# A hybrid decoder layer in fp32: the second feed-forward product done as seven block products instead of eight

## The chip, the core and the metric

One core of a Trainium2 chip runs the whole layer in one launch. TensorE multiplies 128 x 128 weight tiles with up to 512 columns into PSUM; VectorE (DVE), ScalarE (ACT) and GpSimd (POOL) do the element work between SBUF tiles of 128 partitions, and SyncE (SP) issues the transfers between HBM and SBUF. GpSimd does not touch PSUM in this kernel. The metric is device time of one launch in microseconds, the median of several runs; lower is better.

## What is computed

One decoder layer for a prompt of 2048 tokens and 8 sample tokens, model width 1024, feed-forward width 2816. Cut to what matters here:

```python
x = x + rmsnorm(merged @ p['w_out'], p['g_mix_post'])
hf = rmsnorm(x, p['g_ffn_pre']) @ p['w_ffn_in']                     # 1024 -> 2 * 2816
f = (jax.nn.silu(hf[..., :D_FF]) * hf[..., D_FF:]) @ p['w_ffn_out']  # 2816 -> 1024
x = x + rmsnorm(f, p['g_ffn_post'])
```

Everything ahead of this (state space branch, pooling branch, attention to memory, gates) stays as it is.

## The kernel before

Activations lie transposed: channels on partitions, tokens along the columns. The 2048 tokens are four quarters q of 512 columns. The 8 sample tokens ride along with quarters 0 and 1, four each, so that these are 516 columns wide (`fwidth`, L1261) and are worked in two blocks of 258; quarters 2 and 3 are 512 wide. `SB` pairs the quarters: superblock 0 is quarters 0 and 1, superblock 1 is quarters 2 and 3.

Each fp32 product is made of three TensorE passes over fp32r operands: `split` (L170) makes a rounded part on ACT and the rest on DVE (or on POOL), and the passes are high by high, high by low and low by high. So every loaded operand tile costs one ACT and one DVE instruction before TensorE can use it.

The last 1435 us are three stretches.

**First product, superblock 0 and then 1** (`ffn_in`, L1309, pool "half"). Both quarters of a superblock are multiplied together by a scheme of seven block products (Winograd's form of Strassen): `sums` (L1270) makes seven combinations of the normalized input and stores them to `d_S`, `left` (L1297) loads and splits them into 56 `S` tiles, and for each of the 22 tiles f_ of the feed-forward width `w_pair` (L261) combines the weights on DVE. Superblock 0 uses 22 x 7 x 4 x 3 x 2 = 3696 matmuls of 258 columns, superblock 1 1848 of 512. At the end of each f_, ACT takes the sigmoid, POOL multiplies f0 by it (L1386), DVE multiplies by the other half (L1388), and the two tiles go out to `d_f` (L1389). `take` and `plus` (L1340, L1343) move results out of PSUM between the block products.

**Second product** (`ffn_out`, L1402, pool "down"), the plain way: for each quarter, `load_f` (L1392) brings 22 tiles of f through four `xr` buffers and splits them into `f` tiles; then for each of 8 output tiles m, 22 x 3 matmuls for each of two blocks of columns. The blocks are 258 wide in quarters 0 and 1 and 256 wide in 2 and 3; quarter 3 is done in two halves one after the other, with the weights loaded twice. In all 4 x 8 x 22 x 3 x 2 = 4224 matmuls. Weights `fo` come in chunks of 8, 8 and 6 blocks of 128 x 128 from `in_w_all`, three chunks ahead (`prefetch`, L297, `AHEAD`), through four `wr`, `wh` and `wl` buffers (L281 to L294). The last 8 chunks are split on POOL.

**Finish** of a quarter (`finish`, L1428): the sum of squares gives the norm's scale (`rsqrt_rows`, `spread`), then for 8 tiles DVE multiplies (L1442), POOL or DVE adds the residual loaded from `d_x2` (L1443), and the tile is stored (L1444). It runs in the background of the next quarter: `step` (L221) takes one piece of it, `flush` all that is left.

The order of instructions on each engine is fixed when the kernel is built: a scheduler walks a simulated timeline and takes what is ready, by priority, which is the order of the program unless `tc.high_priority(offset=...)` pulls a part ahead (`URGENT` 300, `LEAD` 700). On the chip each engine works its list strictly in that order. SP issues all transfers in order too, and a transfer whose buffer is not free holds those behind it. A pool that is opened after another has been closed takes the same SBUF: the "down" tiles lie where the "half" tiles were, and each waits for the tiles that it overlaps. `xr`, `tmp`, `wr`, `wh`, `wl` and `rb` are outside of these pools.

## Time and profile before

| | us |
|---|---|
| median of 3 runs | 3132.57 (3129.24 to 3135.39) |
| the profiled execution | 3137.2 |
| its span, first to last instruction | 3135.4 |
| first product, superblock 0, first matmul | 1693.8 |
| last matmul of the first product | 2588.4 |
| last matmul of the second product | 3117.3 |

The mean granted TensorE clock is 0.976 of full speed. The profile counts times from the start of the span. In a row of a timeline the columns are start, duration, engine, line and operation, output and input tiles, shape and count; the bracket is the time that the engine stood idle before it and what ended that. Engines: PE is the matmuls, PEld the weight loads beside them, SPq the issue of transfers. Matmuls are pipelined: their own durations (0.28 us at 258 columns) overlap, so the pace is read from start to start, or from a stretch of the chain and the number of matmuls in it.

### The profile page before, as it was taken

Reading aid. Unit: us, or ns where it says so; the run is one execution under the profiler, and the core shown is the slowest. Engines: PE = TensorE matmul, PEld = TensorE weight load, DVE = VectorE, ACT = ScalarE, POOL = GpSimd, SP = SyncE. Lnnn points to the kernel's source line nnn. Section 1 sums busy time; section 2 is a strip of 40 time slices with the busy share of each in tenths; the row PEclk is TensorE's granted clock in tenths of the full one; section 3 lists DMA queues with packets and bytes.
Section 4 is the critical chain, followed back from the end, with each engine's and each line's share of the span. In section 5 each row is a group of like instructions: output and inputs, shape, how many; then the busy total and the mean of one; then the engine's idle time right before and its main releaser. Section 6 shows DMA issues by size and latency. Waiting matters only on the chain. (4 is left out here: it accounts for less than half of the span.)

```text
span 3135.4 us, 47779 instructions
## 1 busy us (share of the span) xinstructions
PE 2984.2 (95%) x18631; PEld 2671.6 (85%) x18631; DVE 1886.8 (60%) x3121; ACT 1197.7 (38%) x2017; POOL 739.2 (24%) x630
## 2 busy tenths in 40 slices
PE   7989998799999999989996999999999999999997
PEld 6778877689997888878885999998888878999997
DVE  8776756664538645485566855557666654345364
ACT  4532434322445333452333433335333334324343
POOL 2564245532245122450222000000000000011012
PEclk9989999899999999999997999999999999999999
DMA  6344333663434433354374732225222225445575
GB/s 213 110 160 140 121 122 115 165 212 98 126 118 155 129 107 124 122 170 144 101 222 138 230 116 80 82 82 172 85 81 81 81 91 169 154 154 176 156 251 172
DMA packets 205715, 432.78 MB, mean 138 GB/s; under 512 B 47472, under 2 KB 55216, under 8 KB 205488
## 3 DMA queue, kind: packets, MB, share of 16 engines
q1 hardware_dynamic: 205488, 429.72, 44.1%
q8 instruction: 146, 2.39, 0.3%
q14 instruction: 81, 0.66, 0.1%
HBM read 362.82 MB, written 66.49 MB: 137 GB/s over the span
## 5 line engine op out<-in xcount | busy, mean ns | idle before, releaser
L171 ACT ACTIVATE wh<-wr 128x1024 fp32r<-128x1024 f32 (+1 forms) x460 | 458.5, 997 | 1058.0 <-PE pa L117 816.8
L117 PE MATMUL pa<-S,wh 128*128 128x258 f32 (+1 forms) x3696 | 831.2, 321 | 29.2 <-ACT S L171 20.5
L172 DVE TENSOR_TENSOR wl<-wr,wh 128x1024 fp32r<-128x1024 f32 x372 | 432.2, 1163 | 516.8 <-ACT wh L171 503.0
L117 PEld LDWEIGHTS pa<-S,wh 128*128 128x128 f32 x3696 | 615.4, 190 | 87.5 <-ACT S L171 22.0
L117 PE MATMUL pa<-h,wh 128*128 128x512 f32 (+2 forms) x2560 | 664.6, 355 | 18.7 <-ACT tmp L1037 7.4
L117 PE MATMUL pa<-S,wl 128*128 128x258 f32 (+1 forms) x1848 | 586.7, 320 | 0.3 <-DVE wl L172 0.3
L117 PEld LDWEIGHTS pa<-h,wh 128*128 128x128 f32 x2560 | 436.4, 191 | 85.4 <-ACT tmp L1037 7.6
L117 PE MATMUL pa<-br,wh 128*128 128x512 f32 (+2 forms) x1848 | 472.8, 352 | 15.4 <-ACT wh L171 8.6
L117 PE MATMUL pa<-f,wh 128*128 128x258 f32 (+1 forms) x2816 | 470.0, 284 | 5.5 <-ACT f L171 3.2
L117 PE MATMUL pa<-h,wl 128*128 128x512 f32 (+2 forms) x1280 | 419.5, 354 | 0.0
L117 PEld LDWEIGHTS pa<-f,wh 128*128 128x128 f32 x2816 | 401.6, 191 | 7.6 <-ACT f L171 4.3
L117 PEld LDWEIGHTS pa<-S,wl 128*128 128x128 f32 x1848 | 349.7, 189 | 27.4 <-DVE wl L172 0.5
L117 PEld LDWEIGHTS pa<-br,wh 128*128 128x128 f32 x1848 | 312.5, 191 | 63.6 <-ACT wh L171 8.6
L172 POOL TENSOR_TENSOR wl<-wr,wh 128x1024 fp32r<-128x1024 f32 (+1 forms) x88 | 214.3, 2438 | 442.0 <-ACT wh L171 331.2
L117 PE MATMUL pa<-f,wl 128*128 128x258 f32 (+1 forms) x1408 | 313.0, 283 | 4.5 <-DVE wl L172 4.5
L117 PE MATMUL pa<-br,wl 128*128 128x512 f32 (+2 forms) x924 | 296.0, 351 | 0.5 <-DVE wl L172 0.5
L117 PEld LDWEIGHTS pa<-h,wl 128*128 128x128 f32 x1280 | 230.1, 191 | 33.4
L1386 POOL TENSOR_TENSOR tmp<-tmp,ev 128x516 f32<-128x516 f32 (+1 forms) x44 | 59.2, 1345 | 840.1 <-ACT tmp L1385 840.1
L117 PEld LDWEIGHTS pa<-f,wl 128*128 128x128 f32 x1408 | 230.7, 190 | 4.8 <-DVE wl L172 4.8
L117 PEld LDWEIGHTS pa<-br,wl 128*128 128x128 f32 x924 | 164.7, 191 | 23.7 <-DVE wl L172 0.8
L172 DVE TENSOR_TENSOR wl<-wt,wh 128x1024 fp32r<-128x1024 f32 x88 | 107.6, 1223 | 108.3 <-ACT wh L171 108.1
L1341 ACT ACTIVATE ev<-pa 128x258 f32<-128x258 f32 (+1 forms) x198 | 89.3, 454 | 180.0 <-PE pa L117 160.2
(329 smaller groups left out, 3494.1 us busy)
## 6 DMA issues: line engine op xcount, KB each, us to landing
wr<-in_w_all SPq DMA_DIRECT2D x408, 512.0 KB, 3.6
ops<-d_ops SPq DMA_DIRECT2D x112, 256.0 KB, 3.8
xr<-in_x_t SPq DMA_DIRECT2D x80, 256.0 KB, 3.7
xr<-d_x SPq DMA_DIRECT2D x72, 256.0 KB, 4.0
wr<-in_w_all SPq DMA_DIRECT2D x40, 384.0 KB, 3.3
d_f<-tmp SPq DMA_DIRECT2D x44, 258.0 KB, 4.4
xr<-d_f SPq DMA_DIRECT2D x44, 258.0 KB, 3.8
d_f<-tmp SPq DMA_DIRECT2D x44, 256.0 KB, 2.9
```

Source lines behind the costliest of these rows:

```text
L117: self._done(self.nc.tensor.matmul(*a, **k))
L171: S.activation(dst_hi, src, AF.Copy)
L172: (eng or V).tensor_tensor(dst_lo, src, f(dst_hi), SUB)
L1341: both(lambda u, s: S.activation(dst[:, s], X[u][:, :w], AF.Copy))
L1386: G.tensor_tensor(f0[:, :n], f0[:, :n], p1[:, :n], MUL)
```

## The change

The second product of a superblock is done as a two-by-two block product in seven products instead of eight: the rows of blocks are the two quarters, the inner blocks the two halves of the feed-forward width (11 tiles each), the columns of blocks the two halves of the model width (4 tiles each).

- **The products** (`ffn_out`): for each superblock, seven products in the order 0, 1, 5, 4, 6, 2, 3, each of 4 output tiles by 11 inner tiles by 3 passes. In superblock 0 each is two matmuls of 258 columns, in superblock 1 one of 512; only the last product of superblock 1 is done in two halves of 256, with its weights loaded twice. Partial results stay in 16 `z` tiles: product 0 is copied out by ACT, the others are added on DVE (`plus`); the squares for the norm are taken by ACT from SBUF and added on POOL, in the last product on DVE.
- **Sums of f** (end of `ffn_in`): the first product now walks f_ as j, j + 11, and after every pair POOL makes four combinations from the tiles at hand (one after the even tile, three after the odd one), 2 a tile on average, 88 in all. They are stored to `d_fs`, late: after the first block product of the next f_ (`put_sums`).
- **Sums of the weights** (`out_weights`): in the background of superblock 1's first product, 11 pieces of 512 columns; each loads four blocks through the four `xr` buffers, makes four combinations on POOL (44 in all) and stores four to `d_T`.
- **Loading** (`load_f`): 11 tiles for each product instead of 22 for each quarter; the loads of the next product are woven in, three after each output tile. The first product's loads are pulled ahead by `LEAD`.
- **Weights**: key `w2`, in chunks of 8 blocks (the last of 4), 6 a product, from `in_w_all` for products 0 to 2 and from `d_T` for the others. The last 6 chunks are split on POOL.
- **Finish**: quarter 0 (or 2) is finished after product 2, beside product 3; quarter 1 beside the next superblock; quarter 3 by halves. Its gain now comes in the multiply (one `scalar_tensor_tensor` on DVE). The residual of quarter 3 is loaded once for both halves into `z` tiles.
- `sums` uses one `tmp` tile less.

```diff
-FCH = (8, 8, 6)
-FOFF = (0, 8, 16)
+KF = NF // 2
+NPC = 4 * KF
+FPC = tuple(min(8, NPC - c) for c in range(0, NPC, 8))
+FORD = tuple(x for j in range(KF) for x in (j, j + KF))
+OUT_ORDER = (0, 1, 5, 4, 6, 2, 3)
+OUT_BLOCK = {0: (0, 0), 1: (1, 0), 2: (1, 1)}
+OUT_SUM = {4: 0, 5: 1, 6: 2, 2: 3}
 SB = ((0, 1), (2, 3))
 KH = KD // 2
...
     wo = [("wo", m) for m in range(KD)]
-    fo = [("fo", c, m) for m in range(KD) for c in range(len(FCH))]
...
     for sb in range(len(SB)):
-        seq += [("f1", f) for f in range(NF)]
-    for q in range(NQ):
-        seq += fo
-    seq += fo
+        seq += [("f1", f) for f in FORD]
+    for sb in range(len(SB)):
+        for i in OUT_ORDER:
+            seq += [("w2", i, c) for c in range(len(FPC))] * len(out_halves(sb, i))
     return seq
 
 
+def out_halves(sb, i):
+    if sb == 0:
+        return [[(0, HW_ // 2), (HW_ // 2, HW_ // 2)]]
+    return [[(0, TQ // 2)], [(TQ // 2, TQ // 2)]] if i == OUT_ORDER[-1] else [[(0, TQ)]]
...
-            "ev": 4, "S": 56, "f": 52, "z": 8}
+            "ev": 4, "S": 56, "f": 44, "z": 16, "st": 3}
...
+    d_fs = dram([len(SB), 4, KF, P, HW_], "d_fs")
+    d_T = dram([4, len(FPC), P, KD * P], "d_T")
...
+        elif key[0] == "w2":
+            src = d_T[key[1] - 3, key[2]] if key[1] > 2 else I["w_all"][_WIDX[("fo",) + OUT_BLOCK[key[1]] + key[2:]]]
...
-        split(hi[:, :n], lo[:, :n], raw[:, :n], G if key[0] in ON_POOL or i >= len(seq) - KD else V)
+        split(hi[:, :n], lo[:, :n], raw[:, :n], G if key[0] in ON_POOL or i >= len(seq) - len(FPC) else V)
...
-            s1, s2, s3, s4 = (slot("tmp")[:, :n] for _ in range(4))
+            s1, s2, s4 = (slot("tmp")[:, :n] for _ in range(3))
+            s3 = A[1, 0]
...
-        for f_ in range(NF):
+        late = []
+
+        def put_sums():
+            for i, j, t in late:
+                nc.sync.dma_start(d_fs[sb, i, j, :, :n], t[:, :n])
+            late.clear()
+
+        for at, f_ in enumerate(FORD):
...
             if nb == 2:
                 product(X, 0, B11, True)
                 take(p1)
+                put_sums()
                 product(Z, 1, B21, True)
...
+            j = at // 2
+            if at % 2 == 0:
+                a21, s3 = f1, slot("tmp")
+                G.tensor_tensor(s3[:, :n], f0[:, :n], f1[:, :n], SUB)
+                late.append((2, j, s3))
+            else:
+                G.tensor_tensor(a21[:, :n], a21[:, :n], f1[:, :n], ADD)
+                G.tensor_tensor(s3[:, :n], f1[:, :n], s3[:, :n], SUB)
+                G.tensor_tensor(f0[:, :n], f0[:, :n], s3[:, :n], SUB)
+                late += [(0, j, a21), (1, j, s3), (3, j, f0)]
             step()
-
-    def load_f(q, n):
-        ft = []
-        for f_ in range(NF):
+        put_sums()
+
+    def out_weights():
+        for c in range(len(FPC)):
+            for o in range(0, FPC[c] * P, 512):
+                W = []
+                for r in range(2):
+                    for m in range(2):
+                        t = slot("xr")
+                        nc.sync.dma_start(t[:, :512], I["w_all"][_WIDX[("fo", r, m, c)]][:, o:o + 512])
+                        W.append(t[:, :512])
+                b11, b12, b21, b22 = W
+                G.tensor_tensor(b22, b22, b12, SUB)
+                G.tensor_tensor(b12, b12, b11, SUB)
+                G.tensor_tensor(b11, b11, b22, ADD)
+                G.tensor_tensor(b21, b21, b11, SUB)
+                yield
+                yield
+                for i, t in enumerate((b21, b12, b11, b22)):
+                    nc.sync.dma_start(d_T[i, c, :, o:o + 512], t)
+                for _ in range(3):
+                    yield
+
+    def load_f(sb, i, out):
+        n = fwidth(SB[sb][0])
+        for k in range(KF):
+            if i in OUT_SUM:
+                src = d_fs[sb, OUT_SUM[i], k]
+            else:
+                src = d_f[SB[sb][i // 2], k + KF * (i > 0)]
             raw = slot("xr")
-            nc.sync.dma_start(raw[:, :n], d_f[q, f_, :, :n])
+            nc.sync.dma_start(raw[:, :n], src[:, :n])
             hi, lo = slot("f", F32R), slot("f", F32R)
             split(hi[:, :n], lo[:, :n], raw[:, :n])
-            ft.append((hi, lo))
-        return ft
-
-    def ffn_out(ft, bl, z, st):
+            out.append((hi, lo))
+            yield
+
+    def ffn_out(sb, i, ft, bl, C, st, loader):
+        u, c11, c12, c22 = C
         sl = slice(bl[0][0], bl[-1][0] + bl[-1][1])
-        for m in range(KD):
+
+        def plus(dst, src, ps):
+            for p_, (o, nn) in zip(ps, bl):
+                V.tensor_tensor(dst[:, o:o + nn], src[:, o:o + nn], p_[:, :nn], ADD)
+
+        def squares(row, t):
+            if st[row] is None:
+                st[row] = slot("st")
+                S.activation(st[row][:, :fwidth(SB[sb][0])], t[:, :fwidth(SB[sb][0])], AF.Square)
+                return
+            sq = slot("tmp")
+            S.activation(sq[:, sl], t[:, sl], AF.Square)
+            (G if sb == 0 or i != 3 else V).tensor_tensor(st[row][:, sl], st[row][:, sl], sq[:, sl], ADD)
+
+        for m in range(KH):
             ps = [psum() for _ in bl]
-            for c in range(len(FCH)):
-                hi, lo = wget("fo", c, m)
-                for j in range(FCH[c]):
-                    i = FOFF[c] + j
-                    ws = slice(j * P, (j + 1) * P)
-                    ah, al = ft[i]
-                    for p_, (o, nn) in zip(ps, bl):
-                        T.matmul(p_[:, :nn], lhsT=hi[:, ws], rhs=ah[:, o:o + nn], start=i == 0, stop=False)
-                        T.matmul(p_[:, :nn], lhsT=hi[:, ws], rhs=al[:, o:o + nn], start=False, stop=False)
-                    for p_, (o, nn) in zip(ps, bl):
-                        T.matmul(p_[:, :nn], lhsT=lo[:, ws], rhs=ah[:, o:o + nn], start=False, stop=i == NF - 1)
-            if len(z) <= m:
-                z.append(slot("z"))
-            sq = st if m == 0 else slot("tmp")
-            for p_, (o, nn) in zip(ps, bl):
-                zs = slice(o, o + nn)
-                S.activation(sq[:, zs], p_[:, :nn], AF.Square)
-                S.activation(z[m][:, zs], p_[:, :nn], AF.Copy, scale=g_fpost[:, m:m + 1])
-            if m > 0:
-                V.tensor_tensor(st[:, sl], st[:, sl], sq[:, sl], ADD)
+            for k in range(KF):
+                c, j = divmod(m * KF + k, 8)
+                if j == 0:
+                    wpiece[0] = wget("w2", i, c)
+                hi, lo = wpiece[0]
+                ws = slice(j * P, (j + 1) * P)
+                ah, al = ft[k]
+                for p_, (o, nn) in zip(ps, bl):
+                    T.matmul(p_[:, :nn], lhsT=hi[:, ws], rhs=ah[:, o:o + nn], start=k == 0, stop=False)
+                    T.matmul(p_[:, :nn], lhsT=hi[:, ws], rhs=al[:, o:o + nn], start=False, stop=False)
+                for p_, (o, nn) in zip(ps, bl):
+                    T.matmul(p_[:, :nn], lhsT=lo[:, ws], rhs=ah[:, o:o + nn], start=False, stop=k == KF - 1)
+            fast.append(tc.high_priority(offset=URGENT if sb and i == 3 else 0))
+            fast[-1].__enter__()
+            if i == 0:
+                u.append(slot("z"))
+                for p_, (o, nn) in zip(ps, bl):
+                    S.activation(u[m][:, o:o + nn], p_[:, :nn], AF.Copy)
+            elif i == 1:
+                c11.append(slot("z"))
+                plus(c11[m], u[m], ps)
+                squares(0, c11[m])
+            elif i == 5:
+                plus(u[m], u[m], ps)
+            elif i == 4:
+                c12.append(slot("z"))
+                plus(c12[m], u[m], ps)
+            elif i == 6:
+                c22.append(slot("z"))
+                plus(c22[m], c12[m], ps)
+                plus(u[m], u[m], ps)
+                squares(1, c22[m])
+            elif i == 2:
+                plus(c12[m], c12[m], ps)
+                squares(0, c12[m])
+            else:
+                plus(u[m], u[m], ps)
+                squares(1, u[m])
+            fast.pop().__exit__(None, None, None)
+            for _ in range(3):
+                next(loader, None)
             step()
+
+    wpiece = [None]
+    fast = []
+    last_x = []
...
-            xt = slot("xr")
-            load_half(xt, d_x2[:, k], q)
+            if q + 1 < NQ:
+                xt = slot("xr")
+                load_half(xt, d_x2[:, k], q)
+            elif len(last_x) > k:
+                xt = last_x[k]
+            else:
+                xt = slot("z")
+                last_x.append(xt)
+                load_half(xt, d_x2[:, k], q)
             zk = z[k][:, sl]
-            V.tensor_tensor(zk, zk, rb, MUL)
+            V.scalar_tensor_tensor(zk, zk, g_fpost[:, k:k + 1], rb, MUL, MUL)
             (V if q + 1 == NQ and k % 2 else G).tensor_tensor(zk, zk, xt[:, sl], ADD)
             nc.sync.dma_start(O["y_t"][q, :, k, sl.start:e], z[k][:, sl.start:e])
             if own(q):
...
         if sb + 1 < len(SB):
             background.append(second_scale(NQ - 1))
             background.append(sums(sb + 1))
+        else:
+            background.append(out_weights())
         ffn_in(sb, got)
         flush()
     second.__exit__(None, None, None)
 
     down = tc.tile_pool(name="down", bufs=1, reuse_waits="tile")
     stage[0] = down.__enter__()
-    slot("z")
-    for q in range(NQ):
-        n = fwidth(q)
-        ft = load_f(q, n)
-        z = []
-        st = slot("tmp")
-        for bl in ([[(0, n // 2), (n // 2, n // 2)]] if q + 1 < NQ else [[x] for x in HALVES]):
-            ffn_out(ft, bl, z, st)
-            flush()
-            background.append(finish(q, z, st, bl))
+    for tag in ("f", "z", "st"):
+        slot(tag)
+    plan = [(sb, i) for sb in range(len(SB)) for i in OUT_ORDER]
+    ft = []
+    with tc.high_priority(offset=LEAD):
+        run(load_f(*plan[0], ft))
+    for at, (sb, i) in enumerate(plan):
+        if i == OUT_ORDER[0]:
+            C, st = ([], [], [], []), [None, None]
+        nxt = []
+        loader = load_f(*plan[at + 1], nxt) if at + 1 < len(plan) else iter(())
+        for bl in out_halves(sb, i):
+            ffn_out(sb, i, ft, bl, C, st, loader)
+            if i == 2:
+                background.append(finish(SB[sb][0], C[1] + C[2], st[0], bl))
+            elif i == 3:
+                flush()
+                background.append(finish(SB[sb][1], C[0] + C[3], st[1], bl))
+        run(loader)
+        ft = nxt
     flush()
     down.__exit__(None, None, None)
 
```

## Rows read from the trace of the kernel before

**Rows 1.** The page, part 1: busy time, share of the span, instructions.
```profile
PE 2984.2 (95%) x18631; PEld 2671.6 (85%) x18631; DVE 1886.8 (60%) x3121; ACT 1197.7 (38%) x2017; POOL 739.2 (24%) x630
```

**Rows 2.** The chain that ended last, in time: start us, us, what.
```profile
2173.09 411.75 PE pa L117 x1776
...
2585.58 2.83 PE pa L117 x11
...
2617.19 124.55 PE pa L117 x1036
2741.75 0.85 PE pb L117 x12
...
2749.31 1.30 PE pb L117 x12
2750.61 120.30 PE pa L117 x1001
...
2879.79 115.54 PE pa L117 x975
```

**Rows 3.** Busy time by stretch: from:to, its length, busy us (instructions), clock, DMA.
```profile
core 0: us, PE busy (x) PEld busy (x) DVE busy (x) ACT busy (x) POOL busy (x), PEclk, DMA share, GB/s
1800.00:2100.00 300.00, 300.00 (x2510) 300.00 (x2510) 166.61 (x278) 109.46 (x194) 19.89 (x15) 1.00 0.32 91
2250.00:2550.00 300.00, 300.00 (x1297) 243.13 (x1296) 186.85 (x233) 99.85 (x138) 19.39 (x15) 1.00 0.25 81
2590.00:2617.00 27.00, 23.03 (x152) 21.38 (x152) 16.54 (x24) 13.31 (x22) 1.32 (x1) 0.87 0.76 223
2592.00:2596.00 4.00, 2.30 (x10) 2.31 (x11) 3.46 (x6) 0.58 (x2) 0.00 (x0) 0.56 0.87 285
2996.00:3061.00 65.00, 60.45 (x491) 60.25 (x491) 42.39 (x54) 27.84 (x40) 13.13 (x8) 0.95 0.71 233
3061.00:3117.00 56.00, 56.00 (x477) 56.00 (x476) 24.70 (x43) 22.38 (x32) 20.35 (x12) 1.00 0.58 191
```

**Rows 4.** Timeline of POOL and of DVE in the first product, superblock 1.
```profile
2224.95 1.29 POOL L1386 TENSOR_TENSOR tmp<-tmp,ev 128x512 f32<-128x512 f32 x1 [18.17 <-ACT tmp L1385]
2244.41 1.30 POOL L1386 TENSOR_TENSOR tmp<-tmp,ev 128x512 f32<-128x512 f32 x1 [18.17 <-ACT tmp L1385]
...
2243.36 0.69 DVE L172 TENSOR_TENSOR wl<-wr,wh 128x512 fp32r<-128x512 f32 x1 [6.93 <-ACT wh L171]
2243.97 0.68 DVE L1380 TENSOR_TENSOR tmp<-tmp,pa 128x512 f32<-128x512 f32 x1
2244.69 1.57 DVE L1388 TENSOR_TENSOR tmp<-tmp,ev 128x512 f32<-128x512 f32 x1
```

**Rows 5.** Instructions by line and shape from 1700 on: count, busy, mean ns, idle before.
```profile
L172 DVE TENSOR_TENSOR wl<-wr,wh 128x1024 fp32r<-128x1024 f32 x118 | 145.3, 1231 | 135.9 <-ACT wh L171 135.8
...
L172 DVE TENSOR_TENSOR f<-xr,f 128x516 fp32r<-128x516 f32 x44 | 29.4, 694 | 16.2 <-ACT f L171 16.0
...
L1442 DVE TENSOR_TENSOR z<-z,rb 128x516 f32<-128x516 f32 x16 | 20.9, 1378 | 1.2 <-ACT rb L372 1.2
```

**Rows 6.** Timeline of DVE where the first product ends.
```profile
2591.38 1.66 DVE L1388 TENSOR_TENSOR tmp<-tmp,ev 128x512 f32<-128x512 f32 x2
```

**Rows 7.** Timeline of DVE beside quarter 3's first half: quarter 2 is finished.
```profile
3006.73 11.48 DVE L1442 TENSOR_TENSOR z<-z,rb 128x512 f32<-128x512 f32 x8
3018.14 2.28 DVE L172 TENSOR_TENSOR wl<-wr,wh 128x1024 fp32r<-128x1024 f32 x1
```

**Rows 8.** Timeline of the tail, after the last matmul of the second product.
```profile
3117.33 0.38 ACT L1422 ACTIVATE tmp<-pa 128x256 f32<-128x256 f32 x1 [7.04 <-PE pa L117]
...
3122.83 2.74 DVE L1442 TENSOR_TENSOR z<-z,pb 128x256 f32<-128x256 f32 x8 [1.18 <-PE pb L117]
...
3132.38 0.42 DVE L1443 TENSOR_TENSOR z<-z,xr 128x256 f32<-128x256 f32 x1 [2.41 <-DMA xr<-d_x]
```

**Rows 9.** Transfers between 2996 and 3061.
```profile
DMA packets 5587, 15.12 MB, mean 233 GB/s; under 512 B 625, under 2 KB 625, under 8 KB 5582
```

More of the change, by code (lines that the diff above doesn't have):

```diff
@@ L81, in _weight_plan @@
     for sb in range(len(SB)):
-        seq += [("f1", f) for f in range(NF)]
-    for q in range(NQ):
-        seq += fo
-    seq += fo
-    return seq
+        seq += [("f1", f) for f in FORD]
+    for sb in range(len(SB)):
+        for i in OUT_ORDER:
+            seq += [("w2", i, c) for c in range(len(FPC))] * len(out_halves(sb, i))
+    return seq
+def out_halves(sb, i):
+    if sb == 0:
+        return [[(0, HW_ // 2), (HW_ // 2, HW_ // 2)]]
+    return [[(0, TQ // 2)], [(TQ // 2, TQ // 2)]] if i == OUT_ORDER[-1] else [[(0, TQ)]]
 _SEQ = _weight_plan()
-_STORED = [k for k in dict.fromkeys(_SEQ) if k[0] not in ("KT", "V", "f1")]
+_STORED = [k for k in dict.fromkeys(_SEQ) if k[0] not in ("KT", "V", "f1", "w2")]
 _STORED += [(k, f) for f in range(NF) for k in ("fa", "fb")]
+_STORED += [("fo", r, n, c) for c in range(len(FPC)) for r in range(2) for n in range(2)]
 _WIDX = {k: i for i, k in enumerate(_STORED)}
@@ L97, in _ncols @@
         return NB * P
-    if key[0] == "fo":
-        return FCH[key[1]] * P
+    if key[0] == "w2":
+        return FPC[key[2]] * P
     return KD * P
@@ L1601, in _pack @@
         else:
-            o = FOFF[key[1]] * P
-            v = kt(a["w_ffn_out"][0][o:o + FCH[key[1]] * P, key[2] * P:(key[2] + 1) * P])
+            _, r, n, c0 = key
+            v = []
+            for t in range(8 * c0, 8 * c0 + FPC[c0]):
+                m, k = n * KH + t // KF, r * KF + t % KF
+                v.append(a["w_ffn_out"][0][k * P:(k + 1) * P, m * P:(m + 1) * P])
+            v = np.concatenate(v, axis=1)
         w_all[i, :, :v.shape[1]] = v
```

3 lines of the change are left out of this document (2 added, 1 removed).

## Prediction

> **What bounds the kernel now.** I read the page first: matmuls fill 95% of the span, DVE 60%, POOL 24% [rows 1]. Then the chain of waits: over the last third it is matmul after matmul, broken only at seams [rows 2]. So TensorE's stream sets the time, and what counts is the number of matmuls, their pace and the holes. The chain gives the pace: 124.55 / 1036 = 0.1202 us a matmul of 258 columns, 115.54 / 975 = 0.1185 at 256, 411.75 / 1776 = 0.2318 at 512 [rows 2]; 512 columns in one matmul are 2% cheaper than in two. Busy time by stretch shows that inside the stages TensorE never stops while DVE is at 56% (superblock 0) and 62% (superblock 1) and POOL at 6 to 7% [rows 3].
>
> The holes of the second product come from the same views. The last matmul of the first product ends at 2588.4, the tail begins at 3117.3 [rows 2, 8]: 528.9 us. Its 4224 matmuls at the two paces are 2112 x 0.1202 + 2112 x 0.1185 = 504.1, and the small matmuls of the finishes 2.15 for a quarter, 7 for all with the shorter later ones [rows 2]. That leaves 17.8 us of holes. At the start, 2588.4 to 2617.2, 152 matmuls ran [rows 3], worth 18.3 of 28.8: 10.5 lost, partly to a halved clock (granted 0.56 from 2592 to 2596, the low level being 1.2 GHz) after TensorE had stood. The rest, some 7, is mostly one seam at 2996 to 3061: 4.5 us idle and a clock of 0.95 [rows 3]. There DVE does quarter 2's eight multiplies in one burst of 11.5 us, the weight split behind it is done only at 3020.4, itself stretched to 2.28 us from 1.23 [rows 5, 7], and in halves a chunk of weights lasts only 8 x 3 x 0.1185 = 2.8 us, three chunks 8.5: less than the burst.
>
> **What is removed.** After the change superblock 0 takes 7 x 4 x 11 x 3 x 2 = 1848 matmuls of 258: 222.1 us. Superblock 1 takes 792 of 512, 183.6, and 264 of 256, 31.3. With the same 7 us for the finishes: 444.0 against 511.1. So **67.1 us** leave the bounding engine, of which 63 are the eighth product. I take the paces as they are: the first product already uses both forms with as many weight loads.
>
> **Start of the second product.** 11 tiles of f instead of 22, pulled ahead. But the "down" tiles lie on the "half" tiles, and `f` now comes first, over `wt` and `ev` (sizes from the code): tiles k = 2 and 3 cover the `ev` buffers, which the last multiplies of the first product read until 2593.0 [rows 6]. So TensorE can run k = 0 and 1, then waits from about 2590 for a split of some 1.4 us (ACT, then DVE 0.69 [rows 5]) behind 2593.0: 4 us, and after standing the clock may fall as it did. Bounds 4 to 11; I take **7**, 3.5 less than now.
>
> **Added to the first product, on POOL.** 88 sums of f and 44 of weights; a POOL operation of this size takes 1.30 us [rows 4]. In superblock 1 that is 4 a tile f_ beside the one there: 6.5 us of a period of 2244.41 - 2224.95 = 19.5 [rows 4]. POOL holds that. What it does to DVE is the point: while POOL ran from 2244.41 to 2245.71, a DVE multiply of two SBUF tiles took 1.57 instead of 0.69, an operation that reads PSUM kept its 0.68 [rows 4, 5]. So an added POOL operation costs DVE up to 0.88 us if it meets such work: 4 x 0.88 = 3.5 on 0.62 x 19.5 = 12.1, or 15.6 of 19.5. DVE stays below TensorE and has stretches of 6.9 us of waiting in each period [rows 4], but a PSUM tile may be cleared late now and then. Queued behind: DVE's f0 multiply waits for POOL's product, which can stand behind a piece of `out_weights` (four sums, 5.2 us, which wait for their loads); behind that multiply stand weight splits and `plus`. Not less than nothing, at most about 20 us (0.5 us for each of 44 tiles); I take **4**, as the f1 weights are split a whole tile ahead. The sums are needed only in the next stage, and their stores go out one block product later, so SP's queue does not wait on POOL; the loads and stores for the weights use `xr`, idle there, with transfers at 0.25 of the engines' time [rows 3].
>
> The Trainium skill, "GPSIMD Engine Reference", 1. Specifications, says that GpSimd shares its SBUF interfaces with VectorE and contends with DVE instructions of two SBUF inputs; the 1.57 us agrees. Taken to its end (all of 132 x 1.3 = 172 us taken from DVE, an estimate by that page) DVE would stand at 89% in superblock 1, which changes no term but is what the last rival prices.
>
> **Inside the second product.** Splits of f rise from 88 to 154 (ACT and DVE, 0.69 each on DVE [rows 5]), weight columns fall from 112,640 to 84,480 (1.23 per 1024), adds out of PSUM are new (56, about 0.8 each). A product lasts 31 us; DVE does 11 x 0.69 + 5.5 x 1.23 + 4 x 0.8 = 18 of it. A finish adds 11 us of multiplies (1.38 each beside POOL [rows 5]) and 3 of norm: 32, about the product's length. Such finishes fall beside product 3 of superblock 0, product 0 of superblock 1, and product 3 of superblock 1. In the first two a chunk lasts 5.6 to 5.8 us, so three ahead cover the burst: 2 us each at most. The last one runs in halves as now, with three chunks for 8.5 us again and POOL's splits among POOL's adds. I take the 7 that the kernel loses today, 3 for the two seams, and 4 for loads that come closer together: **14**, bounds 4 and 30.
>
> **Tail.** Now 18.1 us from the last matmul to the end of the span, and its last add waits for a transfer of the residual [rows 8]. After: 5.5 to the first multiply as now, plus 0.4 as the add and the square now follow each other; twelve DVE operations of 0.34 to 0.42, some 4.5; 2.6 from the last add's end to the end. 13.0; I take **13.5**, bounds 13 and 18.1 (residual not landed).
>
> **Sum**, against the profiled execution's span of 3135.4: 2588.4 + 4 + 7 + 444.0 + 14 + 13.5 = 3070.9, that is 64.5 less. The profiled execution stands 4.6 above the median of the runs (3137.2 to 3132.57) and 1.8 of it lies outside the span, which the change leaves; the gain goes off the median: 3132.57 - 64.5 = **3068**. All low bounds: 2588.4 + 0 + 4 + 444 + 4 + 13 = 3053.4, so 3050.6 us. All high: 2588.4 + 20 + 11 + 444 + 30 + 18.1 = 3111.5, so 3108.7.
>
> **Rivals.**
> - *The second product starves.* The same bytes and more DVE work go into 85% of the time. In the last product of superblock 1 about 11.6 MB must move (weights twice 2.9 less what was fetched ahead, quarter 2's residual and result, quarter 3's residual, half its result) in 31.3 us of matmuls, 370 GB/s, where the busiest long stretch moved 233 [rows 9]. At 233 this is 50 us instead of 31.3 + 13.5: 5 late, and as much at each of the two other finishes, with the clock falling at each (3 us as at 2996 [rows 3]): 20 to 45 us given back, 3088 to 3113. For it: the stall of [rows 7] exists already. Against it: stretches in between have DVE at 58%, so the spill is absorbed.
> - *Nothing waits.* Seams covered, first product untouched: 3042 to 3050.
> - *The gain does not come* (the product is not shorter, because the paces rise as the number falls): to give 67.1 us back, 2904 matmuls would have to be 23 ns slower each; the first product's pace speaks against it. 3125 to 3140.
> - *Slower: POOL stops the first product.* If every added POOL operation's 0.88 us lands on TensorE, not on DVE's idle time, 132 x 0.88 = 116 us are lost: 3068 - 4 + 116 = 3180. It decides from 0.52 us an operation on (68.5 / 132). It needs DVE without slack; the 6.9 us of waiting in each period [rows 4] speak against it.
>
> The Trainium skill, "HBM Reference", Specifications (TRN2), gives about 425 GB/s to a core that streams alone. By it the 370 GB/s of the first rival would fit and its transfer part be nothing; no stretch of this length in the trace comes near, so I keep the rival.
>
> **How the numbers follow.** Forecast (3050 to 3088) 0.68; starving (3088 to 3113) 0.20; nothing waits 0.06; gain does not come 0.02; slower 0.04. The range takes in the forecast, and the starving case up to 3100, which leaves out some 0.18: 3049 to 3100. 0.2%, or 6 us, is about what a measurement tells from no change. Faster 0.94, same 0.02, slower 0.04.
>
> **What would show it.** Matmuls on the tile `f`: 1848 of 258, 792 of 512, 264 of 256, at the same paces. The last matmul on `S` at most 10 us later than 2588.4. DVE multiplies of L1388's kind longer than 0.69 in more places, POOL near 33% in superblock 1. The first `f` product idle near 4 us. The stall in the last product as now. Tail 13 to 14 us without a wait for the residual. Wrong if TensorE shows idle time inside the first product, or several us at each product of the second.

## The result

The changed kernel takes 3098.35 us (median of 4 runs, 3095.52 to 3101.12) against 3131.81 for the kernel before on the same chip (3129.24 to 3135.39): a ratio of 0.9892 (95% interval 0.9875 to 0.9909). It is faster, as the interval lies below 1, and inside the stated range, but the gain is 33.5 us where 64.5 were forecast. The profiled execution has a span of 3093.7.

The table splits each profiled execution at four events read from the timeline of TensorE: the first matmul on a tile `S`, the first one of 512 columns on `S` (superblock 1 begins), the start of the last one on `S`, and the start of the last matmul on `f`. "Second" is from the last `S` to the last `f`, the tail from there to the end. The start of the first product itself lies between 1686 and 1701 in these executions, though next to nothing ahead of it was changed; so spans differ by that, and the columns are compared, not the spans. A column is one execution each: where kernels share an edit, theirs differ by up to 2.4 us. The medians of e1 to e10 were taken beside runs of the kernel before with medians of 3135.05 to 3136.09.

| kernel | start | superblock 0 | superblock 1 | second | tail | span | median of its runs |
|---|---|---|---|---|---|---|---|
| before | 1693.8 | 458.3 | 436.1 | 528.8 | 18.4 | 3135.4 | 3131.81 |
| after | 1686.1 | 463.4 | 461.2 | 466.6 | 16.4 | 3093.7 | 3098.35 |
| e1_no_wsum | 1693.5 | 464.6 | 441.6 | 467.9 | 16.4 | 3084.0 | 3084.35 |
| e2_no_fsum | 1692.2 | 459.5 | 452.0 | 467.8 | 16.6 | 3088.1 | 3087.48 |
| e3_neither | 1700.6 | 457.7 | 437.9 | 468.4 | 16.5 | 3081.1 | 3076.46 |
| e4_wtraffic | 1692.6 | 464.5 | 443.4 | 466.5 | 16.8 | 3083.8 | 3086.40 |
| e5_pool_only | 1689.0 | 463.1 | 453.5 | 467.3 | 16.6 | 3089.5 | 3096.74 |
| e6_pinned | 1691.5 | 462.2 | 440.4 | 467.9 | 16.6 | 3078.6 | 3083.18 |
| e7_finish_behind | 1695.4 | 462.7 | 441.2 | 467.8 | 15.3 | 3082.4 | 3083.70 |
| e8_late_stores | 1698.6 | 460.4 | 436.6 | 468.2 | 16.8 | 3080.6 | 3082.20 |
| e9_all | 1696.9 | 462.7 | 437.0 | 466.6 | 16.0 | 3079.2 | 3077.78 |
| e10_later | 1692.5 | 461.6 | 437.4 | 458.3 | 22.1 | 3071.9 | 3079.42 |

From before to after: second product -62.2, tail -2.0, superblock 0 +5.1, superblock 1 +25.1. That is -34.0 without the accident of the start, and the medians say -33.5. The second product gave what was forecast; the first product took half of it back.

The page of the changed kernel, part 1, to be read against [rows 1]: TensorE works 61 us less, POOL 254 more.

```profile
PE 2922.8 (94%) x17311; PEld 2570.1 (83%) x17311; DVE 1999.4 (65%) x3220; ACT 1186.1 (38%) x1973; POOL 993.1 (32%) x784
```

Busy time by stretch, columns as in [rows 3]: superblock 0, the seam between the superblocks, superblock 1, the start of the second product, two stretches inside it, and its end.

```profile
1800.00:2100.00 300.00, 299.86 (x2507) 299.66 (x2506) 190.55 (x283) 108.94 (x195) 69.33 (x46) 1.00 0.40 121
2150.00:2180.00 30.00, 25.00 (x122) 20.43 (x121) 23.89 (x37) 14.80 (x25) 10.67 (x4) 0.94 0.71 207
2250.00:2550.00 300.00, 287.55 (x1214) 230.31 (x1214) 197.68 (x223) 93.28 (x131) 115.60 (x74) 0.98 0.45 155
2612.00:2632.00 20.00, 15.53 (x100) 14.73 (x101) 13.65 (x17) 9.18 (x16) 5.88 (x4) 0.83 0.74 228
2632.00:2818.00 186.00, 186.00 (x1551) 186.00 (x1549) 110.85 (x159) 87.37 (x130) 15.60 (x10) 1.00 0.62 199
2864.00:3037.00 173.00, 172.77 (x773) 141.28 (x774) 105.79 (x132) 77.67 (x111) 27.12 (x18) 1.00 0.67 213
3037.00:3062.00 25.00, 18.64 (x159) 18.43 (x157) 23.39 (x31) 7.27 (x9) 18.55 (x9) 0.95 0.62 199
3062.00:3077.00 15.00, 11.84 (x83) 11.87 (x84) 13.14 (x30) 2.10 (x5) 10.22 (x9) 0.74 0.28 90
```

In its long stretches the second product runs at 186.0 / 1551 = 0.120 us a matmul without a hole, DMA at 199 to 213 GB/s. In the first product TensorE stops in two of the stretches shown, the seam and superblock 1. The waits between 2180 and 2360 (who waits, for whom, us in total, times, longest) say why:

```profile
POOL xr L1438 <- DMA xr<-in_w_all: 64.4, 10, 13.7
ACT ev L1364 <- POOL tmp L1411: 55.7, 7, 11.1
DVE tmp L1413 <- POOL tmp L1411: 46.0, 8, 11.1
...
PE pa L128 <- ACT ev L1364: 8.0, 4, 2.7
...
PE pa L128 <- DVE wl L183: 4.4, 3, 2.1
```

L1438 is the first of the four weight sums of a piece, L1411 POOL's sigmoid product, L1413 the multiply of the two halves, L1364 `take`. The scheduler had put all 11 pieces of `out_weights` close together: their sums begin every 15.4 us on average, from 2191 to 2345. They share the four `xr` buffers, so each piece is load, four sums, store, and then the next load. POOL stands in front of the next piece's first sum until its load is in, and the sigmoid product, whose data are ready, stands behind it in POOL's list. The timeline of one such place, two tiles f_ long, with [rows 4] as its picture before:

```profile
2238.04 1.29 POOL L1438 TENSOR_TENSOR xr<-xr,xr 128x512 f32<-128x512 f32 x1 [6.81 <-DMA xr<-in_w_all]
...
2242.03 1.28 POOL L1411 TENSOR_TENSOR tmp<-tmp,ev 128x512 f32<-128x512 f32 x1
...
2243.35 0.60 ACT L1364 ACTIVATE ev<-pa 128x512 f32<-128x512 f32 x1 [7.24 <-POOL tmp L1411]
2243.35 1.77 DVE L1413 TENSOR_TENSOR tmp<-tmp,ev 128x512 f32<-128x512 f32 x1 [8.58 <-POOL tmp L1411]
...
2260.33 0.60 ACT L1364 ACTIVATE ev<-pa 128x512 f32<-128x512 f32 x1 [7.56 <-POOL tmp L1411]
...
2260.98 1.22 PE L128 MATMUL pa<-S,wh 128*128 128x512 f32 x2 [2.73 <-ACT ev L1364]
```

In the first tile POOL waits 6.81 for a load, and ACT and DVE wait 7.24 and 8.58 for POOL (the `ev` buffer that `take` wants to write is still to be read by POOL and DVE); TensorE still has work and does not stop. One tile later ACT waits 7.56 for POOL again, PSUM is not cleared, and TensorE stops for 2.73. The Trainium skill, "Perfetto Trace Analysis", Tensor Engine Instruction (MATMUL, LD_WEIGHTS), says that ACT, DVE and GPSIMD work strictly first in, first out; the 64.4 us of POOL's waiting, with finished inputs queued behind it, agree.

### The profile page after: what moved, and what is told of

It is laid out like the page before. It is cut to its first block, busy times and chain, and to the rows that moved or that the text cites. A ratio compares the mean times of both kernels' runs of the same rounds, so it can differ in the third digit from the quotient of the medians.

```text
span 3093.7 us, 45909 instructions
## 1 busy us (share of the span) xinstructions
PE 2922.8 (94%) x17311; PEld 2570.1 (83%) x17311; DVE 1999.4 (65%) x3220; ACT 1186.1 (38%) x1973; POOL 993.1 (32%) x784
## 5 line engine op out<-in xcount | busy, mean ns | idle before, releaser
L182 ACT ACTIVATE wh<-wr 128x1024 fp32r<-128x1024 f32 (+1 forms) x430 | 427.8, 996 | 894.4 <-PE pa L128 647.0
L183 DVE TENSOR_TENSOR wl<-wr,wh 128x1024 fp32r<-128x1024 f32 x344 | 422.9, 1230 | 259.7 <-ACT wh L182 248.6
L128 PE MATMUL pa<-br,wh 128*128 128x512 f32 (+2 forms) x1848 | 471.6, 351 | 15.3 <-ACT wh L182 8.9
L128 PE MATMUL pa<-f,wh 128*128 128x258 f32 (+2 forms) x1936 | 399.7, 315 | 5.4 <-DVE f L183 2.9
L183 POOL TENSOR_TENSOR wl<-wr,wh 128x1024 fp32r<-128x1024 f32 x86 | 211.8, 2466 | 435.4 <-ACT wh L182 343.2
L128 PEld LDWEIGHTS pa<-f,wh 128*128 128x128 f32 x1936 | 299.0, 191 | 29.8 <-DVE f L183 3.4
L128 PE MATMUL pa<-f,wl 128*128 128x258 f32 (+2 forms) x968 | 254.3, 315 | 0.0
L183 DVE TENSOR_TENSOR wl<-wt,wh 128x1024 fp32r<-128x1024 f32 x88 | 124.2, 1411 | 90.4 <-ACT wh L182 90.4
L1364 ACT ACTIVATE ev<-pa 128x258 f32<-128x258 f32 (+1 forms) x198 | 87.5, 455 | 245.5 <-PE pa L128 172.8
L1411 POOL TENSOR_TENSOR tmp<-tmp,ev 128x516 f32<-128x516 f32 (+1 forms) x44 | 62.1, 1412 | 369.4 <-ACT tmp L1410 369.3
L128 PEld LDWEIGHTS pa<-f,wl 128*128 128x128 f32 x968 | 162.8, 190 | 11.5
```

The lines of the kernel that those rows point to most:

```text
L128: self._done(self.nc.tensor.matmul(*a, **k))
L182: S.activation(dst_hi, src, AF.Copy)
L183: (eng or V).tensor_tensor(dst_lo, src, f(dst_hi), SUB)
L1364: both(lambda u, s: S.activation(dst[:, s], X[u][:, :w], AF.Copy))
L1411: G.tensor_tensor(f0[:, :n], f0[:, :n], p1[:, :n], MUL)
```

## The experiments

Three questions: what in the added work costs the first product its 30 us, whether it can be had without that, and what the stall near the end is made of. In e1 to e5 parts of the arithmetic are left out, as their expectations say; e6 to e10 compute the layer.

### Which part costs it: weights, f, or both

e1_no_wsum takes the weight blocks as they are in the input and makes no sums of them:

```diff
-            src = d_T[key[1] - 3, key[2]] if key[1] > 2 else I["w_all"][_WIDX[("fo",) + OUT_BLOCK[key[1]] + key[2:]]]
+            src = I["w_all"][_WIDX[("fo",) + OUT_BLOCK[key[1] % 3] + key[2:]]]
...
-        else:
-            background.append(out_weights())
```

> The changed kernel without the sums of the weights in the first product; products 3 to 6 read stored blocks of the weights instead of sums, so the output is not the reference's. The stretch from the first to the last matmul on S took 894.6 us before and 924.7 after. Theory 'queue' (the weight sums stand in POOL's list ahead of the sigmoid product and wait there for their loads; DVE, ACT and then TensorE wait behind): some 17 us of the 30 go, stretch 904 to 910, about 3078 to 3084 us. Rival 'port' (POOL's work slows DVE whatever its order; 44 of 132 added operations go): a third, 10 us, goes, stretch 913 to 916, about 3088.

e2_no_fsum makes no sums of f and loads tiles of `d_f` in their place:

```diff
-            j = at // 2
-            if at % 2 == 0:
-                a21, s3 = f1, slot("tmp")
-                G.tensor_tensor(s3[:, :n], f0[:, :n], f1[:, :n], SUB)
-                late.append((2, j, s3))
-            else:
...
-                src = d_fs[sb, OUT_SUM[i], k]
+                src = d_f[SB[sb][i % 2], k + KF * (i > 4)]
```

> The changed kernel without the 88 sums of f and their stores; every product loads plain tiles of f instead, so the output is not the reference's. Theory 'queue': the weight sums still hold the sigmoid product, so only the losses of superblock 0 and of the seam at 2150 to 2180 go, 8 to 11 us: stretch 913 to 917, about 3087 to 3090. Rival 'port' (88 of 132 operations go): two thirds of the loss go, stretch 903 to 907, about 3078.

e3_neither does both edits.

> The changed kernel with neither sums of the weights nor sums of f; the output is not the reference's. Both theories: the whole loss of the first product goes, stretch 893 to 898, so that what is left is the second product in seven: about 3066 to 3072 us. If the stretch stays above 905, something else in the changed first product (the order of f, one tmp tile less) costs time.

Measured: without weight sums superblock 1 falls from 461.2 to 441.6; without sums of f it falls to 452.0 and superblock 0 from 463.4 to 459.5; without both the stage is back at 895.6 against 894.4 before. So the added sums are the loss, to within 1.2 us. The whole first product takes 906.2 in e1, where "queue" said 904 to 910, and 911.5 in e2, between what "port" and "queue" said. The sums of f alone cost some 6 in each superblock (e1 against before), the weight sums alone 16 in superblock 1 (e2 against before), both together 25 there. That is 4 more than the two alone; that they share POOL's list would explain it, but no run shows it.

Superblock 0's part lies near its start. From 50 to 110 us behind the first matmul TensorE ran 504 matmuls before and 467 after, 37 x 0.1202 = 4.4 us; in the 100 us from 210 on both ran 839. First the row of before, then that of after:

```profile
1743.80:1803.80 60.00, 60.00 (x504) 60.00 (x504) 52.09 (x88) 22.28 (x39) 5.13 (x3) 1.00 0.72 222
```

```profile
1736.10:1796.10 60.00, 57.63 (x467) 57.18 (x466) 48.58 (x75) 20.87 (x37) 12.95 (x8) 0.97 0.68 207
```

DVE is busy there for 52 of 60 us even before. Whether POOL's list or its slowing of DVE costs the time here was not tested, and e6 to e10 leave 2 to 4 us of it (460.4 to 462.7 against 458.3).

### What about the weight sums: transfers, POOL's work, or order

e4_wtraffic keeps loads and stores and drops the four POOL operations of each piece:

```diff
-                G.tensor_tensor(b22, b22, b12, SUB)
-                G.tensor_tensor(b12, b12, b11, SUB)
-                G.tensor_tensor(b11, b11, b22, ADD)
-                G.tensor_tensor(b21, b21, b11, SUB)
```

> The changed kernel with the loads and the stores of the weight sums, but without their 44 operations on POOL, so the output is not the reference's. The stretch from the first to the last matmul on S was 924.8 us after the change, 906.6 without any of it. 'Queue' (POOL's list waits for the loads in front of the sigmoid product): nothing is left in POOL's list that waits, stretch 905 to 909, 3080 to 3086 us. Rival 'traffic' (the 23 MB beside the weights' own loads delay these): stretch 918 to 925, about 3096 to 3100.

Measured: superblock 1 takes 443.4, within 2 us of the kernel without weight sums. The 23 MB that go in and come out cost next to nothing by themselves. "Traffic" is out: the first product takes 907.9, where "queue" said 905 to 909.

e5_pool_only makes the 44 POOL operations on four blocks that are loaded once, with no further load and no store:

```diff
-        for c in range(len(FPC)):
-            for o in range(0, FPC[c] * P, 512):
...
+        W = []
+        for r in range(2):
+            for m in range(2):
+                t = slot("xr")
+                nc.sync.dma_start(t[:, :512], I["w_all"][_WIDX[("fo", r, m, 0)]][:, :512])
+                W.append(t[:, :512])
+        for _ in range(11):
+            b11, b12, b21, b22 = W
...
-                for i, t in enumerate((b21, b12, b11, b22)):
-                    nc.sync.dma_start(d_T[i, c, :, o:o + 512], t)
```

> The changed kernel with the 44 operations of the weight sums on POOL, all on the same four tiles that are loaded once, and without the other loads and the stores; products 3 to 6 read stored blocks, so the output is not the reference's. 'Queue': POOL works as much but waits for no load, so most of the 18 us go: stretch 906 to 914, about 3081 to 3090 us. Rival 'port' (what POOL's operations take from DVE): the loss stays, stretch 918 to 925, about 3096 to 3100.

Measured: 453.5 in superblock 1, a whole first product of 916.6, between what the theories said, so this run alone decides nothing. Its waits from 2180 to 2360 show that the edit had not taken the queue away. The 44 operations now stood in one burst, with the first load still ahead of them, and the sigmoid product waited among them:

```profile
ACT ev L1364 <- POOL tmp L1411: 19.2, 3, 8.2
DVE tmp L1413 <- POOL tmp L1411: 17.6, 5, 5.1
POOL xr L1437 <- DMA xr<-in_w_all: 13.6, 1, 13.6
```

e6_pinned keeps all work and all bytes of the change. A piece now takes three steps instead of five, and a tile f_ has three, so about one piece falls to a tile. It puts each piece's first sum behind the latest sigmoid product and each further sum behind the last one, two steps after the loads were issued. The dependence fixes the order in POOL's list and adds no semaphore:

```diff
-            G.tensor_tensor(f0[:, :n], f0[:, :n], p1[:, :n], MUL)
+            behind[0] = G.tensor_tensor(f0[:, :n], f0[:, :n], p1[:, :n], MUL).ins.name
...
+    def pinned(r):
+        tc.add_manual_dep(r.ins, behind[0], mybir.DependencyInfo(
+            mybir.DependencyClass.NoSync, mybir.DependencyReason.DATA), reason="order")
+        behind[0] = r.ins.name
...
-                G.tensor_tensor(b22, b22, b12, SUB)
...
                 yield
+                yield
+                pinned(G.tensor_tensor(b22, b22, b12, SUB))
...
-                for _ in range(3):
-                    yield
```

> The changed kernel with all of its work, but the four sums of a piece of the weights are ordered behind the sigmoid product of the tile f_ in which their loads were issued, one piece a tile. Theory 'queue': the sums no longer wait in front of the sigmoid product, the 17 us go although POOL does the same work: stretch 905 to 911, about 3079 to 3085 us, faster than before and after. Rival 'port' and a rival 'traffic' (the added transfers delay the weights): same operations and transfers, nothing gained, stretch 920 to 926, 3095 to 3100.

Measured: superblock 1 takes 440.4, no more than without any weight sums (441.6 in e1), and the kernel runs at 0.9834 of before (0.9819 to 0.9849). Its waits in the same stretch: the 64.4 us of POOL for loads are 2.4, the 55.7 of `take` for POOL 0.5.

```profile
POOL xr L1448 <- DMA xr<-in_w_all: 2.4, 3, 1.1
...
ACT ev L1364 <- POOL tmp L1411: 0.5, 1, 0.5
```

The stretch 2180 to 2360 by busy time, first of before, then of after, then of e6_pinned:

```profile
2180.00:2360.00 180.00, 180.00 (x779) 145.88 (x778) 113.41 (x142) 61.24 (x86) 11.64 (x9) 1.00 0.27 86
```

```profile
2180.00:2360.00 180.00, 167.55 (x695) 133.02 (x695) 123.15 (x128) 56.35 (x80) 99.21 (x67) 0.97 0.68 228
```

```profile
2180.00:2360.00 180.00, 180.00 (x777) 145.96 (x777) 153.47 (x145) 62.25 (x89) 107.48 (x61) 1.00 0.65 217
```

In these 180 us after runs 84 matmuls fewer than before, 84 x 0.2318 = 19.5 us; TensorE stood for 12.45 of them, and its granted clock was 0.97 instead of 1.00. e6 has nearly as many POOL operations as after (61 and 67) and nearly the same traffic, DVE is busy for 153 of 180 us, and TensorE never stops. So in superblock 1 neither the bytes nor POOL's work beside DVE stops TensorE; where the weight sums stand in POOL's list, and wait there, does. e6 changes three things at once: the sums' place behind the sigmoid product, the lead of their loads, and their spacing (a piece in 19.4 us instead of 15.4). Which of them would be enough alone was not tested.

### The sums of f: a store that waits in SP's queue

At the seam the trace of after shows TensorE stopping three times, the longest:

```profile
2174.43 0.97 PE L128 MATMUL pa<-S,wh 128*128 128x512 f32 x3 [2.78 <-ACT S L182]
```

Behind the `S` tile stands its load, L1319, and SP issues in order. The waits of SP's queue from 2140 to 2190 show three stores of `d_fs` (L1333) waiting for POOL, with the loads of `d_S` behind them:

```profile
SPq L1333 <- POOL tmp L1421: 4.4, 1, 4.4
...
SPq L1333 <- POOL tmp L1423: 3.1, 1, 3.1
...
SPq L1333 <- POOL tmp L1422: 0.9, 1, 0.9
```

Inside the superblocks the stores go out a block product later; SP waits at them there too (54.5 us in 10 waits for L1423 between 1690 and 2140), but past the first 160 us TensorE keeps its pace beside that. Those of superblock 0's last tile, however, go out at once. e8_late_stores is e6_pinned with these three stores issued behind the loads of `d_S`:

```diff
+                r = nc.sync.dma_start(d_fs[b, i, j, :, :w_], t[:, :w_])
+                if b != sb:
+                    tc.add_manual_dep(r.ins, last_S[0], mybir.DependencyInfo(
+                        mybir.DependencyClass.NoSync, mybir.DependencyReason.DATA), reason="order")
...
-        put_sums()
+        if sb + 1 == len(SB):
+            put_sums()
```

> The kernel with the weight sums ordered behind the sigmoid product (e6), and in addition the last three stores of sums of f of superblock 0 issued behind the loads of S for superblock 1. After the change SP stood up to 4.4 us at such a store, waiting for POOL, with loads of S behind it, and TensorE idled 2.8 and 0.9 us there. Theory 'store in the queue': 3 to 6 us less in the first product, stretch 897 to 900 instead of 903.0. Rival (the loads of S are late anyway, as before the change, and DVE's splits set the seam): within 2 us, 901 to 905.

Measured: 460.4 and 436.6; the first product takes 897.0, 2.6 more than before. The seam, 40 us from the first matmul of 512 columns on, first in after, then in e8:

```profile
2149.50:2189.50 40.00, 35.00 (x166) 28.53 (x165) 30.21 (x46) 20.80 (x36) 10.67 (x4) 0.96 0.71 210
```

```profile
2159.00:2199.00 40.00, 38.60 (x190) 31.78 (x189) 36.18 (x53) 24.60 (x40) 13.43 (x6) 1.00 0.76 234
```

In the same 40 us before runs 192 matmuls, e6 and e7 run 173 and 170. The median is 1 us below that of e6, which is not to be told from it; the column shows what the median cannot. e9 and e10 below have the same edit and repeat it: superblock 1 takes 436.6, 437.0 and 437.4 with the late stores, 440.4 and 441.2 without (e6, e7), which is 3.0 to 4.6 us, and the first product takes 897.0, 899.7 and 899.0, where "store in the queue" said 897 to 900.

### The stall near the end

In after TensorE stands still for 9.53 us in the last product, in front of the small matmul over the squares of quarter 3's first half. The rows of TensorE and of DVE:

```profile
3065.16 0.99 PE L128 MATMUL pb<-ones,st 128*128 128x1 f32 x4 [9.53 <-DVE st L1478]
```

```profile
3045.79 15.33 DVE L1550 SCALAR_TENSOR_TENSOR z<-z,gv,rb 128x512 f32<-128x512 f32 x8
3061.04 1.48 DVE L1478 TENSOR_TENSOR st<-st,tmp 128x256 f32<-128x256 f32 x1
```

Quarter 2's eight multiplies are one burst, as in [rows 7], but of 15.33 us instead of 11.48, and the add of squares stands behind it. After standing, the granted clock of the last 15 us is 0.74. e7_finish_behind is e6_pinned with the multiplies ordered behind the adds:

```diff
+            r = V.scalar_tensor_tensor(zk, zk, g_fpost[:, k:k + 1], rb, MUL, MUL)
+            if q == NQ - 2:
+                tc.add_manual_dep(r.ins, last_add[0], mybir.DependencyInfo(
+                    mybir.DependencyClass.NoSync, mybir.DependencyReason.DATA), reason="order")
```

> The kernel with the weight sums ordered behind the sigmoid product (e6), and in addition the eight multiplies with which quarter 2 is finished ordered behind the last adds of squares of the last product's first half. In e6 TensorE stood 9.5 us at the small matmul on st, which came after those eight multiplies, 15.3 us on DVE, and its clock fell after that. Theory 'burst' (that stall is the multiplies in front of the add of squares): the stall goes, the tail grows by up to 5 as the multiplies end later: 5 to 11 us less than e6, 3072 to 3078. Rival (the last product is bound by POOL's splits of the weights or by transfers, and the stall only hides that): within 3 us of e6, 3080 to 3086.

Measured: the gain did not come. The second product takes 467.8 as in e6. The median lies where the rival put it, but not for the rival's reason: the stall moved to the next small matmul of the same norm, whose DVE chain now stood behind the six multiplies that were left, 13.5 us:

```profile
3060.16 1.19 PE L128 MATMUL pb<-tmp,ones 128*128 128x128 f32 x4 [10.86 <-DVE tmp L377]
```

e9_all is e6, e7 and e8 together.

> The three orders together: weight sums behind the sigmoid product, superblock 0's last stores of sums of f behind the loads of d_S, quarter 2's multiplies behind the adds of squares. If each of them is worth what it was worth alone (first product 897, second product 468, tail 15.3), the span is 2588.2 - 894.4 + 897 + 468 + 15.3 = 3074 to 3081 with the start of the first product at 1686 to 1701, and the median is about 3081, one below the kernel with late stores: not to be told from it. If the order of the multiplies also frees the second product once the first is shorter, the second product falls below 463.

Measured: 3077.78 (3073.74 to 3080.98), 0.9816 of before (0.9802 to 0.9831). That is not to be told from e8 (0.9826, 0.9812 to 0.9841). The multiplies' order did not free the second product here either: 466.6.

e10_later is e8 with the norm of that half begun two output tiles later, so that 47 more matmuls stand ahead of it in TensorE's list:

```diff
-    def finish(q, z, st, bl):
+    def finish(q, z, st, bl, later=0):
+        for _ in range(later):
+            yield
...
-                background.append(finish(SB[sb][1], C[0] + C[3], st[1], bl))
+                background.append(finish(SB[sb][1], C[0] + C[3], st[1], bl,
+                                         2 if sb and bl == out_halves(sb, i)[0] else 0))
```

> As with late stores, and the norm of quarter 3's first half is begun two output tiles later, so that TensorE has 47 more matmuls (5.6 us) ahead of the matmul over the squares that stood 9.5 us. If the stall near the end is only this place in TensorE's list (theory 'list'), some 4 of the 9.5 us are left, the clock falls less, and the second product is 459 to 463 instead of 468; the tail grows by 0 to 4, as the first half's multiplies now fall into it. If DVE is simply full there (theory 'full': quarter 2's 15.3 us of multiplies also hold the splits of weights and the adds out of PSUM), TensorE stands as long at another place, a split or a pa tile, and the second product stays at 466 to 469.

Measured: the second product takes 458.3, 9.9 less than e8. The tail takes 22.1 instead of 16.8, more than the 0 to 4 expected, as the first half's multiplies now lie in it. In the last 40.3 us up to the last matmul on `f` TensorE runs 296 matmuls at a granted clock of 0.96, in e8 247 at 0.87 (first e8, then e10):

```profile
3023.50:3063.80 40.30, 30.77 (x247) 30.60 (x246) 37.18 (x60) 9.41 (x15) 28.82 (x17) 0.87 0.51 159
```

```profile
3009.50:3049.80 40.30, 38.04 (x296) 37.08 (x295) 34.38 (x45) 13.37 (x19) 27.64 (x15) 0.96 0.55 171
```

It no longer stands in front of the squares; it waits 2.26 for a weight split and 3.08 at the second small matmul, which now lies in the tail:

```profile
3038.34 0.58 PE L128 MATMUL pa<-f,wl 128*128 128x256 f32 x1 [2.26 <-POOL wl L183]
3053.17 0.68 PE L128 MATMUL pb<-tmp,ones 128*128 128x128 f32 x4 [3.08 <-DVE tmp L377]
```

So what stopped TensorE was the place of the small matmul in its list: for the second product "list" holds and "full" falls, and with it e7's rival. But DVE is busy for 17.09 of the last 17.8 us of the second product there, and about half of what is gained comes back in the tail. What the whole is worth stays open: second product and tail together are 4.6 less than e8's, while the median of 3079.42 comes from runs between 3073.72 and 3088.76.

## Why the prediction was half right

**The range: met by luck.** 3098.35 lies in 3049 to 3100 only because the range was widened to 3100 for the starving rival, whose mechanism did not occur. The forecast itself, 3050 to 3088, was missed by 10 us, and the prediction's own sign of being wrong came: TensorE stood inside the first product, for 12.45 us between 2180 and 2360 alone.

**What is removed: right.** Matmuls on `f` are 1936 on `wh` and 968 on `wl`, 2904 as counted, at 0.120 us for 258 columns. The second product takes 466.6 where 7 + 444.0 + 14 = 465 was the sum.

**Start: right in size.** From 2610.7 to 2632 TensorE ran 102 matmuls, worth 102 x 0.1202 = 12.3 of 21.3 us: 9.0 lost, bounds 4 to 11, value 7. It stood 2.44 and 2.71 us for splits of f, and the clock was 0.84.

**Inside the second product: right in sum, not in place.** 466.6 - 444.0 - 9.0 leaves 13.6 for 14. I had put 7 at the last finish, 3 at two other seams and 4 on loads. Nearly all is the last finish: from 3037 to 3077.3 there were 244 matmuls, at 0.1185 some 28.9 of 40.3 us, 11.4 lost. The other seams are almost closed (from 2818 to 2864 TensorE is busy for 45.12 of 46 us), and loads cost nothing (172.77 of 173). And the mechanism was another: I named the weight split behind the burst, it was the small matmul of the norm.

**Tail: 16.1 from the end of the last matmul, as the prediction counts it, between the bounds, value 13.5.** The bound "residual not landed" is what happened. SP issued seven stores of the result first, the load of the last residual tile stood behind them, and DVE and POOL waited for it:

```profile
3077.74 3.28 SPq L1552 DMA_DIRECT2D out_y_t<-z  x7
...
3081.08 0.94 SPq L1280 DMA_DIRECT2D z<-d_x  x2
...
3084.61 0.42 DVE L1551 TENSOR_TENSOR z<-z,z 128x256 f32<-128x256 f32 x1 [1.31 <-DMA z<-d_x]
```

**The step that failed: "Added to the first product, on POOL", 4 with a bound of 20; it measured 30.2.** The mechanism that decided was written down there: the f0 multiply waits for POOL's product, "which can stand behind a piece of `out_weights` (four sums, 5.2 us, which wait for their loads)". Its bound was priced at 0.5 us a tile, and its value at 4 in all, because f1's weights are split a tile ahead. Three things were left out of the price. It holds only if the pieces lie as the program's steps spread them, one for about two tiles f_, while the scheduler put one every 15.4 us; so the wait came at all eight tiles between 2180 and 2360. I took a piece's wait as its four sums; with four buffers in a ring it is store, load and sums, and the longest wait for a load was 13.7 us. And the waiting engine holds not only DVE's multiply but also `ev`, through it `take`, and so PSUM. I also wrote that SP's queue does not wait on POOL because the stores go out a block product later. SP did wait at them, and at superblock 0's last tile, whose stores are not a block product later, it cost 3.0 to 4.6 (e6 and e7 to e8, e9 and e10).

With both orders mended the term is 2.6, 5.3 and 4.6 (e8, e9, e10 against before), and the forecast of 4 would have stood. So the forecast described the work and not its place in the lists. What is left then lies mostly in superblock 0 (2.1 to 4.4), and its cause stays open.

**The rivals.** "The second product starves" fell: TensorE was full beside 199 and 213 GB/s, and in the last product it waited for DVE (9.53 us), not for a transfer. "POOL stops the first product" was the right place with the wrong price. It was 0.88 us an operation through the shared access; measured was 30.2 / 132 = 0.23, and some 24 of the 30.2 came from waiting in line (20.8 in POOL's list, 461.2 to 440.4, and 3.0 to 4.6 in SP's). The prediction's argument against it, DVE's slack, holds in e6 for superblock 1. The 0.5 us per tile and the 20 us were no bound at all: they were one size of the mechanism, not its end.

## What to carry to other kernels

When work is added to an engine that has time, ask first what stands behind it in that engine's list and what it waits for: POOL was at 32% and still took some 20 us from TensorE, because an operation that waited for a transfer stood in front of one whose inputs were ready. Put background work that waits for transfers behind the operation that the critical engine needs, and issue its loads a step earlier: the two together gave the 20 us back here. The same holds of a queue of transfers (a store that waits for a slow engine holds the loads behind it) and of TensorE's own list (a small matmul with a long chain ahead of it belongs behind work that is ready).

## What the hardware showed beside this

The slowing of DVE and POOL goes both ways. In e6 DVE lost (153.47 - 113.41) / (61 - 9) = 0.77 us for each POOL operation added, near the 0.88 of [rows 4]. But that is an average over unlike operations: in e4, with 18 sums of f more than before and no weight sums, DVE's time in the same 180 us is 113.69, as before. Operations with both inputs in SBUF lost: the four that combine the weights (L278 to L281 in e6) rose from 0.68 or 0.69 us to between 1.21 and 1.61. Those that read PSUM (L1367) kept their time, 0.681 before and 0.677 in e6; the prediction read that off an operation that met POOL for 0.24 us only, e6 confirms it. POOL's own operation, 1.30 us alone, took 5.79 while DVE worked on two SBUF tiles at the seam of after (the next one began 5.74 us behind it), and 1.6 to 2.4 for most of the weight sums in e6:

```profile
2164.26 5.79 POOL L1421 TENSOR_TENSOR tmp<-tmp,tmp 128x516 f32<-128x516 f32 x1 [5.85 <-DVE tmp L1413]
```

The prediction priced only DVE's side. On POOL the price of an operation depends on what DVE does at that moment, and whoever stands behind it waits for that too.
